# A state chunk's sums kept in one PSUM bank: A S added onto AK V, outputs onto R S, operand copied by ScalarE

## The chip, the cores and the metric

The kernel runs on one core of one Trainium2 chip. The metric is device time in microseconds (us) of one execution. Five engines with queues of their own take part: TensorE (PE in the profile, with its weight loads as PEld), VectorE (DVE), ScalarE (ACT), GpSimd (POOL) and SyncE (SP), which issues most transfers. Each runs its instructions in the order in which they stand in its queue. TensorE writes to PSUM, whose banks the kernel names by tags ("d" and "g" and "ry" two buffers each, "tr" and "sas" one each).

## The reference, cut to what matters

One layer takes an input of 1024 tokens by 1024 channels, projects it, and runs three branches: an RWKV-7 recurrence with 16 heads of 64 channels, a convolution of width 31, and a cross-attention into 256 memory tokens. The branches are merged by gates and projected again. The change lies in the recurrence, and in the group normalisation behind it:

```
def step(state, inp):
    r_t, w_t, k_t, v_t, a_t, b_t = inp
    sa = jnp.einsum('bhvk,bhk->bhv', state, a_t)
    state = (state * w_t[:, :, None, :]
             + sa[..., :, None] * b_t[:, :, None, :]
             + v_t[..., :, None] * k_t[:, :, None, :])
    y = jnp.einsum('bhvk,bhk->bhv', state, r_t)
    return state, y
...
mu = jnp.mean(wkv, axis=-1, keepdims=True)
var = jnp.mean(jnp.square(wkv - mu), axis=-1, keepdims=True)
wkv = ((wkv - mu) * lax.rsqrt(var + RWKV_GN_EPS)).reshape(B, S, RWKV_WIDTH)
```

## The kernel before

The recurrence is computed in chunks of 64 tokens. A tile j holds two heads (128 channels); its 1024 tokens are two halves e of 512, and a half is 8 chunks, in two quarters q of 4. In each chunk the kernel needs, besides products within the chunk, the state S (128x128, two heads on the diagonal) from the chunk before. The instructions come from four kinds of Python generators:

- tile jobs (`g_dense`, L298): the projections. A half tile is 24 matmuls with 512 columns into a "d" bank, then a few operations on it (L379 to L385, L427), the split of weights into a high and a low part (L123 on ScalarE, L124 on VectorE; `wh`, `wl`), and the load of the next weights.
- `g_prep`: decays, keys and queries of a half, with `ar` and `bk` as its results, and the products of the chunk against itself (L552, masked on VectorE by L555).
- `g_sub`: the inversion of a triangular matrix for all chunks of a half. The masked products go through DRAM (`ud`, L560, L573), GpSimd scales them (L581, `U`), and a loop of 31 steps on VectorE (L587 and L590, `W`) does the inversion; the result goes through DRAM again and becomes `TT`.
- `g_chain`: the recurrence over the 8 chunks of a half. In `g_pre`, per quarter, K and V are transposed (L640, L647, bank "tr"); AK V (L666) goes to the second half of that bank, and ScalarE copies it to `Y` (L675). Then, per chunk: R S and A S in one matmul (L709, `ry`), VectorE adds A S and AK V to `sav` (L710), ScalarE scales the old state (L713, `sp`), TensorE makes the update (L717, `sas`), VectorE joins both (L720, `s`). After four chunks the outputs' own part (L731, `yp`) goes to a "tr" bank, ScalarE copies it to `Y` (L733), VectorE adds R S (L738), and takes statistics (L742). At the end of a half, small operations (L750 to L755), a reciprocal square root on GpSimd (L114, L118, `vr`), two normalising operations (L760, L761), a transposition on TensorE (L766), two more VectorE operations (L768, L769) and a store.

`mix()` interleaves the generators, by the shares of their steps that are done, so that TensorE has projection matmuls between the steps of the recurrence. A compiler pass then gives every engine its order, by its own estimate of when things are ready; it is fixed when the kernel runs. So a change in one generator moves instructions of the others.

The stretch of the profile from about 60 to 990 us is this recurrence stage. It repeats with a period of one tile j, that is two chains (e = 0 and e = 1), some 114 us. The text calls "X" the half period from the transposition L766 that ends a chain e = 1 to the one that ends the chain e = 0 (in the period shown: 479.25 to 535.01 us), and "Y" the other half.

Of the kernel before, what the change touches and what calls it, by code (L numbers as in the profile page):

```python
# [13 lines left out]
ALU = mybir.AluOpType  # L14
# [4 lines left out]
P = 128  # L19
# [5 lines left out]
C = 64  # L25
# [7 lines left out]
RMS_EPS = 1e-6  # L33
LN_EPS = 1e-5
GN_EPS = 64e-5
PAIR_EVERY = 34.0
TAP = 1.4
LOS = (13, 14, 15, 16, 17)
# [24 lines left out]
def hybrid_kernel(ctx: ExitStack, tc: tile.TileContext, x: bass.AP, mem: bass.AP, wt: bass.AP,  # L63
                  vecs: bass.AP, wup: bass.AP, gfin: bass.AP, out: bass.AP):
    nc = tc.nc
    act, dve, pool, pe = nc.scalar, nc.vector, nc.gpsimd, nc.tensor
# [7 lines left out]
    def bank(tag, bufs=1):  # L74
        return ps.tile([P, HS], F32, name=tag, tag=tag, bufs=bufs)
# [37 lines left out]
    def rsqrt(out_ap, in_ap, mul, add):  # L113
        pool.tensor_scalar(out=out_ap, in0=in_ap, scalar1=mul, scalar2=add, op0=ALU.mult, op1=ALU.add)  # L114
        p0 = in_ap.shape[0]
        n = in_ap.shape[1]
        base = 0 if p0 == P else P - p0
        pool.tensor_tensor(out=out_ap, in0=out_ap, in1=nhalf[base:P, 0:n], op=ALU.pow)  # L118
# [63 lines left out]
    order = [kinds[n_] + j for lst, _ in schedule for n_, j in lst]  # L182


    def jb(name, *idx):
        return [(name, i) for i in idx]
# [9 lines left out]
    for job in rest[1:]:  # L196
        att_jobs.append(job)
        t_ += cost.get(job[0], 10.2)
        if npair < KT and t_ > npair * PAIR_EVERY:
            att_jobs += jb("gb", npair) + jb("ga", npair)  # L200
# [135 lines left out]
    with tc.tile_pool(name="rk", bufs=1, reuse_waits="tile") as rk:  # L336


        def so(par):
            return 0 if par else C  # L340

        def ko(par):
            return C if par else 0
# [46 lines left out]
        def fl(ap):  # L390
            return ap.rearrange("p a t -> p (a t)")
# [240 lines left out]

        state = [0]

        def g_pre(j, e, q, g, bk, v, Y):
            tkp = bank("tr")
            for cc in range(4):
                pe.transpose(tkp[:, cc * P:(cc + 1) * P], fl(bk[:, q * 4 + cc, :, :]), ident)  # L640
            tk = rk.tile([P, 4, P], F32, name="tk", tag="tk", bufs=2)
            act.copy(tk, tkp.rearrange("p (c t) -> p c t", t=P))
            yield
            vtp = bank("tr")
            for cc in range(2):
                c = q * 4 + cc * 2
                pe.transpose(vtp[:, cc * P:(cc + 1) * P], v[:, c * C:(c + 2) * C], ident)  # L647
            sav = rk.tile([P, 4, P], F32, name="sav", tag="sav", bufs=2)
            for par in range(2):
                rows = slice(ko(par), ko(par) + C)  # L650
                act.copy(sav[rows, par::2, :], vtp[rows, 0:2 * P].rearrange("p (c t) -> p c t", t=P))
            yield
            zv = vtp[:, 2 * P:4 * P]
            u1 = bank("g", 2)
            uv = u1.rearrange("p (k c h t) -> p k c h t", k=2, c=2, h=2)
            for n in range(4):
                cc2, hh = n // 2, n % 2
                vsl = slice(hh * C, (hh + 1) * C)
                for par in range(2):
                    own = slice(so(par), so(par) + C)  # L660
                    oth = slice(ko(par), ko(par) + C)
                    cc = cc2 * 2 + par
                    gc = g[:, par, hh, q * 2 + cc2]
                    pe.matmul(uv[own, 0, cc2, hh, :], lhsT=TT[own, hh * 4 + q * 2 + cc2, :], rhs=tk[own, cc, vsl],
                              start=True, stop=True)
                    pe.matmul(zv[own, n * C:(n + 1) * C], lhsT=gc[oth, own], rhs=sav[oth, cc, vsl],  # L666
                              start=True, stop=True)
            for n in range(4):
                cc2, hh = n // 2, n % 2
                for par in range(2):  # L670
                    own = slice(so(par), so(par) + C)
                    oth = slice(ko(par), ko(par) + C)
                    pe.matmul(uv[own, 1, cc2, hh, :], lhsT=TT[own, hh * 4 + q * 2 + cc2, :],
                              rhs=g[own, par, hh, q * 2 + cc2, oth], start=True, stop=True)
            act.copy(fl(Y[:, q * 2:q * 2 + 2, :]), zv)  # L675
            for par in range(2):
                own = slice(so(par), so(par) + C)
                oth = slice(ko(par), ko(par) + C)
                act.copy(tk[own, par::2, :], uv[own, 0].rearrange("p c h t -> p c (h t)"))
                act.copy(g[own, par, :, q * 2:q * 2 + 2, oth], uv[own, 1].rearrange("p c h t -> p h c t"))  # L680
            yield (tk, sav)

        def g_chain(j, e):
            g, ar, bk, pc = GG.pop((j, e)), AR.pop((j, e)), BK.pop((j, e)), PCS.pop((j, e))
            v = VS.pop((j, e))
            if e == 0:
                dve.memset(s0[state[0]], 0.0)

            Y = rk.tile([P, 4, P], F32, name="Y", tag="Y", bufs=1)
            st = rk.tile([P, 4, 2, 6], F32, name="st", tag="st", bufs=1)  # L690
            pre = [g_pre(j, e, q, g, bk, v, Y) for q in range(2)]
            got = None
            for got in pre[0]:
                yield
# [2 lines left out]
            bv = rk.tile([P, HS], F32, name="bv", tag="bv", bufs=1)  # L697
            dve.tensor_tensor(out=bv, in0=bp, in1=v, op=ALU.mult)
            for q in range(2):
                tk, sav = got  # L700
                ry = bank("ry", 2)
                for cc in range(4):
                    c = q * 4 + cc
                    par = c % 2
                    cg = e * CPH + c
                    own = slice(so(par), so(par) + C)
                    cs = slice(cc * P, (cc + 1) * P)
                    S0, S1 = s0[state[0]], s0[1 - state[0]]
                    pe.matmul(ry[:, cs], lhsT=fl(ar[:, c, :, :]), rhs=S0, start=True, stop=True)  # L709
                    dve.tensor_tensor(out=sav[own, cc, :], in0=ry[own, cs], in1=Y[own, c // 2, :], op=ALU.add)  # L710
                    if cg < NCH - 1:
                        sp = rk.tile([P, P], F32, name="sp", tag="sp", bufs=1)
                        act.activation(sp, S0, AF.Copy, scale=pc[:, c:c + 1])  # L713
                    yield
                    if cg < NCH - 1:
                        sn = bank("sas")
                        pe.matmul(sn[:, 0:P], lhsT=tk[:, cc, :], rhs=sav[:, cc, :], start=True, stop=True)  # L717
                        for hh in range(2):
                            vsl = slice(hh * C, (hh + 1) * C)
                            dve.scalar_tensor_tensor(out=S1[vsl, vsl], in0=sn[vsl, vsl], scalar=pc[vsl, c:c + 1],  # L720
                                                     in1=sp[vsl, vsl], op0=ALU.mult, op1=ALU.add)
                        state[0] = 1 - state[0]
                    if q == 0 and cc < 3:
                        got = next(pre[1])
                    yield
                yp = bank("tr")
                for n in range(4):
                    cc2, hh = n // 2, n % 2
                    for par in range(2):
                        oth = slice(ko(par), ko(par) + C)  # L730
                        pe.matmul(yp[oth, n * C:(n + 1) * C], lhsT=g[:, par, hh, q * 2 + cc2, oth],  # L731
                                  rhs=sav[:, cc2 * 2 + par, hh * C:(hh + 1) * C], start=True, stop=True)
                act.copy(fl(Y[:, q * 2:q * 2 + 2, :]), yp[:, 0:2 * P])  # L733
                yield
                ryv = ry.rearrange("p (c t) -> p c t", t=P)
                for par in range(2):
                    oth = slice(ko(par), ko(par) + C)
                    dve.tensor_tensor(out=Y[oth, q * 2:q * 2 + 2, :], in0=Y[oth, q * 2:q * 2 + 2, :],  # L738
                                      in1=ryv[oth, par::2, :], op=ALU.add)
                for c2 in range(q * 2, q * 2 + 2):  # L740
                    for hh in range(2):
                        dve.bn_stats(out=st[:, c2, hh, :], in_=Y[:, c2, hh * C:(hh + 1) * C])  # L742
                yield
# [11 lines left out]
            dve.scalar_tensor_tensor(out=vr, in0=df, scalar=16.0, in1=vr, op0=ALU.mult, op1=ALU.add)  # L755
            rsqrt(vr, vr, 1.0 / C, GN_EPS)
            for _ in range(GNW):
# [418 lines left out]
    with tc.tile_pool(name="wo1", bufs=1, reuse_waits="tile") as w1:  # L1176
# [12 lines left out]
        for fh in range(2):  # L1189
            fs = slice(fh * HS, (fh + 1) * HS)  # L1190
            oh, ol = wo[fh]
            for t in range(KT):
# [10 lines left out]
                if fh == 1:  # L1203
                    rsqrt(rs[:, t:t + 1], ss[:, t, 1:2], 1.0 / D, e0[:, t:t + 1])
                    for h_ in range(2):
                        hs_ = slice(h_ * HS, (h_ + 1) * HS)
                        dve.scalar_tensor_tensor(out=xr[t][:, hs_], in0=xr[t][:, hs_], scalar=rs[:, t:t + 1],
                                                 in1=gf[:, hs_], op0=ALU.mult, op1=ALU.mult)
# [46 lines left out]
```

## Time and profile before

| | before |
|---|---|
| runs | 1951.31, 1953.14, 1950.67 us; median 1951.31 |
| profiled execution | 1949.77 us, span 1947.8 us, granted clock 0.993 |
| PE busy | 1844.5 us, 95% |
| DVE busy | 1410.6 us, 72% |
| ACT busy | 691.9 us, 36% |
| POOL busy | 227.7 us, 12% |
| DMA, mean | 97 GB/s |

A table like this says which engine has the least room over the whole program. It does not say what a change in one stage is worth; for that the stage's own rows are read, which stand below.

### The profile page before, as it was taken

The page shows a single profiled execution, that of the slowest core. Times are in us where ns is not written, and L with a number is a line of the kernel's source. Part 1 is how long each engine was busy: PE and PEld are TensorE (multiplying, and loading weights), DVE is VectorE, ACT ScalarE, POOL GpSimd, SP SyncE. Part 2 cuts the span into 40 slices and gives each one's busy share as a digit, 9 for nine tenths or more (in the row PEclk, how much of TensorE's full clock was granted, in tenths as well). Part 3 has the DMA queues.
Part 4 walks back from the last instruction along what each step waited for, and adds up shares of the span by engine and source line. Part 5 has one row for each costly group of instructions (what it writes and reads, how often), then busy time and mean ns, then how long its engine had stood idle before and what let it go on. Part 6 is the DMA issues. An engine that isn't in the chain of part 4 may idle for free.

```text
span 1947.8 us, 30024 instructions
## 1 busy us (share of the span) xinstructions
PE 1844.5 (95%) x11412; PEld 1472.2 (76%) x11412; DVE 1410.6 (72%) x3028; ACT 691.9 (36%) x1303; POOL 227.7 (12%) x311
## 2 busy tenths in 40 slices
PE   6999998999899898998999999999999999899998
PEld 5777776766676676776788888888888788778886
DVE  5667787777878777787735998898999857654423
ACT  6334343433344343343333323131313335432121
POOL 2201111111111112111000000000000223100001
PEclk9999999999999999999999999999999999999999
DMA  4232212222121222212224411112122666785432
GB/s 147 57 99 58 77 35 63 60 56 74 42 83 44 62 63 53 77 42 71 69 72 141 130 54 55 65 59 71 44 76 87 227 199 214 246 283 170 129 130 86
DMA packets 127936, 188.61 MB, mean 97 GB/s; under 512 B 64432, under 2 KB 66608, under 8 KB 127792
## 3 DMA queue, kind: packets, MB, share of 16 engines
q1 hardware_dynamic: 122704, 178.11, 29.8%
q10 hardware_dynamic: 4768, 8.07, 1.1%
q8 instruction: 89, 1.46, 0.3%
q0 software_dynamic: 320, 0.52, 0.1%
q14 instruction: 55, 0.45, 0.1%
HBM read 139.92 MB, written 46.20 MB: 96 GB/s over the span
## 4 chain that ended last, share of the span: by engine, by line
PE 63%; DVE 23%; DMA 4%; issue 4%; ACT 3%; POOL 3%; SPq 0%; DVEq 0%; POOLq 0%; ACTq 0%
PE d L298 41%; PE g L298 5%; PE g L212 4%; DVE W L590 3%; DVE tm L587 3%; PE d L212 2%; DVE s L720 2%; PE g L552 2%; DVE wl L124 2%; DVE sav L710 1%; PE ry L894 1%; POOL vr L118 1%; DVE Y L761 1%; DVE Y L738 1%; PE sas L717 1%
## 5 line engine op out<-in xcount | busy, mean ns | idle before, releaser
L298 PE MATMUL d<-hH,wh 128*128 128x512 f32 x1504 | 607.2, 404 | 2.4 <-ACT lc L383 2.0
L298 PE MATMUL d<-hH,wl 128*128 128x512 f32 x1504 | 603.0, 401 | 0.0
L298 PE MATMUL d<-hL,wh 128*128 128x512 f32 x1504 | 600.1, 399 | 0.0
L298 PEld LDWEIGHTS d<-hH,wl 128*128 128x128 f32 x1504 | 285.0, 189 | 56.9
L298 PEld LDWEIGHTS d<-hH,wh 128*128 128x128 f32 x1504 | 285.3, 190 | 55.8 <-ACT lc L383 2.4
L298 PEld LDWEIGHTS d<-hL,wh 128*128 128x128 f32 x1504 | 285.0, 189 | 53.6
L848 DVE SCALAR_TENSOR_TENSOR ac<-up,wdw,ac 128x1024 f32<-128x1024 f32 x240 | 308.0, 1283 | 11.8 <-ACT ac L845 5.9
L123 ACT CAST wh<-wf 128x1024 fp32r<-128x1024 f32 x137 | 143.6, 1049 | 311.3 <-PE d L298 277.1
L124 DVE TENSOR_TENSOR wl<-wf,wh 128x1024 fp32r<-128x1024 f32 x137 | 177.6, 1296 | 83.8 <-ACT wh L123 83.3
L590 DVE TENSOR_TENSOR W<-W,tm 128x60 f32<-128x60 f32 (+24 forms) x496 | 112.3, 226 | 10.0
L587 DVE TENSOR_TENSOR tm<-W,U 128x60 f32<-128x60 f32 (+24 forms) x496 | 107.7, 217 | 11.1
L713 ACT ACTIVATE sp<-s,pc 128x128 f32<-128x128 f32 x120 | 48.3, 402 | 174.8 <-DVE s L720 137.6
L717 PEld LDWEIGHTS sas<-sav,tk 128*128 128x128 f32 x240 | 38.5, 188 | 67.7 <-DVE sav L710 49.4
L717 PE MATMUL sas<-sav,tk 128*128 128x128 f32 x240 | 54.2, 307 | 34.3 <-DVE sav L710 32.6
L720 DVE SCALAR_TENSOR_TENSOR s<-sas,pc,sp 64x64 f32<-64x64 f32 x240 | 67.6, 282 | 21.5 <-PE sas L717 16.1
L298 PE MATMUL g<-oH,wh 128*128 128x512 f32 x192 | 76.3, 398 | 5.3 <-ACT wh L123 5.3
L298 PE MATMUL g<-oH,wl 128*128 128x512 f32 x192 | 76.2, 397 | 2.1 <-DVE wl L124 2.1
L298 PE MATMUL g<-oL,wh 128*128 128x512 f32 x192 | 75.8, 395 | 0.0
L298 PE MATMUL d<-oL,wh 128*128 128x512 f32 x192 | 75.2, 392 | 0.0
L298 PE MATMUL d<-oH,wl 128*128 128x512 f32 x192 | 75.2, 392 | 0.0
L298 PE MATMUL d<-oH,wh 128*128 128x512 f32 x192 | 75.2, 392 | 0.0
L710 DVE TENSOR_TENSOR sav<-ry,Y 64x128 f32<-64x128 f32 x128 | 36.8, 287 | 43.7 <-ACT Y L675 26.8
(301 smaller groups left out, 2910.6 us busy)
## 6 DMA issues: line engine op xcount, KB each, us to landing
wf<-in_wt_dram SPq DMA_DIRECT2D x137, 512.0 KB
g_d<-gt SPq DMA_DIRECT2D x48, 256.0 KB
U<-ud SPq DMA_DIRECT2D x64, 128.0 KB
nxt<-in_x_dram SPq DMA_DIRECT2D x8, 512.0 KB
o_rwkv_d<-o SPq DMA_DIRECT2D x16, 256.0 KB
cv_d<-ac SPq DMA_DIRECT2D x8, 512.0 KB
o_mem_d<-om SPq DMA_DIRECT2D x16, 256.0 KB
xs<-cv_d SPq DMA_DIRECT2D x8, 512.0 KB
```

Source lines behind the costliest of these rows:

```text
L123: act.copy(hi, src)
L124: (eng or dve).tensor_tensor(out=lo, in0=src, in1=hi.bitcast(F32), op=ALU.subtract)
L212: pe.matmul(po, lhsT=l, rhs=r, start=(i == 0), stop=(i == n - 1))
L298: pe.matmul(po, lhsT=l[:, ks_], rhs=r[:, k, sl], start=(n == 0), stop=(n == 3 * KT - 1))
L552: pe.matmul(gps[hh][:, cc * P:(cc + 1) * P], lhsT=fl(bk[rows, c, :, :]), rhs=fl(ar[rows, c, :, :]), start=True, stop=True)
L587: dve.tensor_tensor(out=tv, in0=W[:, 0:m, i:i + 1].broadcast_to([NG * 32, m, n]), in1=U[:, i:i + 1, i + 1:32].broadcast_to([NG * 32, m, n] ...
L590: dve.tensor_tensor(out=wv_, in0=wv_, in1=tv, op=ALU.add)
L710: dve.tensor_tensor(out=sav[own, cc, :], in0=ry[own, cs], in1=Y[own, c // 2, :], op=ALU.add)
L713: act.activation(sp, S0, AF.Copy, scale=pc[:, c:c + 1])
L717: pe.matmul(sn[:, 0:P], lhsT=tk[:, cc, :], rhs=sav[:, cc, :], start=True, stop=True)
L720: dve.scalar_tensor_tensor(out=S1[vsl, vsl], in0=sn[vsl, vsl], scalar=pc[vsl, c:c + 1], in1=sp[vsl, vsl], op0=ALU.mult, op1=ALU.add)
L848: dve.scalar_tensor_tensor(out=ac, in0=up[:, tap:tap + S], scalar=wdw[:, tap * 8 + j:tap * 8 + j + 1], in1=ac, op0=ALU.mult, op1=ALU.add)
```

## The change

In `g_pre`, AK V (L671 of the changed kernel) goes into the `ry` bank and begins the sums there; R S and A S (L716) are added onto it; ScalarE copies A S + AK V to `sav` (L720, act.copy of 64x128), and VectorE's addition is gone. The outputs' own part (L741) is added onto R S in the same bank, and ScalarE copies the sum to `Y` in two pieces of 64x256 (L748); the copy of 128x256 and VectorE's two additions are gone, and so is the copy of AK V. The line numbers behind the first hunk are higher by 1 up to `g_pre`, and by up to 10 behind it. In all:

- removed: 128 additions of 64x128 and 64 of 64x256 on VectorE, 64 copies of 128x256 on ScalarE;
- added: 128 copies of 64x128 and 64 of 64x256 on ScalarE;
- the same matmuls, with other accumulation flags and order; the "tr" bank is used less.

```diff
-            zv = vtp[:, 2 * P:4 * P]
+            ry = bank("ry", 2)
+            first = {}
             u1 = bank("g", 2)
...
-                    pe.matmul(zv[own, n * C:(n + 1) * C], lhsT=gc[oth, own], rhs=sav[oth, cc, vsl],
-                              start=True, stop=True)
+                    mm = pe.matmul(ry[own, cc * P + hh * C:cc * P + (hh + 1) * C], lhsT=gc[oth, own],
+                                   rhs=sav[oth, cc, vsl], start=par not in first, stop=False,
+                                   skip_group_check=True)
+                    if par in first:
+                        tc.add_manual_dep(mm.ins, first[par].name, NOSYNC, reason="sums begun in order")
+                    else:
+                        first[par] = mm.ins
...
-            act.copy(fl(Y[:, q * 2:q * 2 + 2, :]), zv)
...
-                ry = bank("ry", 2)
...
-                    pe.matmul(ry[:, cs], lhsT=fl(ar[:, c, :, :]), rhs=S0, start=True, stop=True)
-                    dve.tensor_tensor(out=sav[own, cc, :], in0=ry[own, cs], in1=Y[own, c // 2, :], op=ALU.add)
+                    mm = pe.matmul(ry[:, cs], lhsT=fl(ar[:, c, :, :]), rhs=S0, start=False, stop=False,
+                                   skip_group_check=True)
+                    for begun in first.values():
+                        tc.add_manual_dep(mm.ins, begun.name, NOSYNC, reason="sums begun in order")
+                    act.copy(sav[own, cc, :], ry[own, cs])
...
-                yp = bank("tr")
...
-                        pe.matmul(yp[oth, n * C:(n + 1) * C], lhsT=g[:, par, hh, q * 2 + cc2, oth],
-                                  rhs=sav[:, cc2 * 2 + par, hh * C:(hh + 1) * C], start=True, stop=True)
-                act.copy(fl(Y[:, q * 2:q * 2 + 2, :]), yp[:, 0:2 * P])
+                        cc = cc2 * 2 + par
+                        pe.matmul(ry[oth, cc * P + hh * C:cc * P + (hh + 1) * C],
+                                  lhsT=g[:, par, hh, q * 2 + cc2, oth], rhs=sav[:, cc, hh * C:(hh + 1) * C],
+                                  start=False, stop=True, skip_group_check=True)
...
-                    dve.tensor_tensor(out=Y[oth, q * 2:q * 2 + 2, :], in0=Y[oth, q * 2:q * 2 + 2, :],
-                                      in1=ryv[oth, par::2, :], op=ALU.add)
+                    act.copy(Y[oth, q * 2:q * 2 + 2, :], ryv[oth, par::2, :])
```

The change moves instructions on every engine. Three places matter for what follows. The first is ScalarE's queue in X, where the first chunk of the chain's second quarter stands (`lc` is a 128x1 operation of a tile job, which needs VectorE's L380 before it). Before:

```order
L713 ACTIVATE sp<-s_1_406,pc 128x128
L495 ACTIVATE e_412<-lw 128x8x64
L496 ACTIVATE lw<-lw 128x512
L733 COPY Y<-tr 128x256
L491 ACTIVATE ta_5194<-g,a0h 128x512
L379 ACTIVATE rs<-d,omm 128x512
L383 ACTIVATE lc<-d,vec 128x1
L123 CAST hsh<-rs 128x512
```

With the change:

```order
L723 ACTIVATE sp<-s_1_406,pc 128x128
L496 ACTIVATE e_412<-lw 128x8x64
L497 ACTIVATE lw<-lw 128x512
L748 COPY Y<-ry 64x256
L492 ACTIVATE ta_5155<-g,a0h 128x512
L748 COPY Y<-ry 64x256
L380 ACTIVATE rs<-d,omm 128x512
L384 ACTIVATE lc<-d,vec 128x1
L720 COPY sav<-ry 64x128
L124 CAST hsh<-rs 128x512
```

The copy of `sav` of that chunk, which was an addition in VectorE's queue, now stands on ScalarE behind `lc`, and the two copies of `Y` stand apart.

The second is GpSimd's queue at the end of Y. Before:

```order
L574 MEMSET W 128x256
L580 COPY W<-rb 32x8 x4
L581 TENSOR_TENSOR U<-U,rb 128x1024
L114 TENSOR_SCALAR vr<-vr 128x8
L118 TENSOR_TENSOR vr<-vr,nhalf 128x8
```

With the change:

```order
L575 MEMSET W 128x256
L581 COPY W<-rb 32x8 x4
L115 TENSOR_SCALAR vr<-vr 128x8
L119 TENSOR_TENSOR vr<-vr,nhalf 128x8
L582 TENSOR_TENSOR U<-U,rb 128x1024
```

The scaling of `U` moved behind the reciprocal square root in Y; in X it stood behind it already.

The third is VectorE's queue at the end of X. Before:

```order
L738 TENSOR_TENSOR Y<-Y,ry 64x256 x2
L742 BN_STATS st<-Y 128x6 x4
...
L754 TENSOR_TENSOR df<-df 128x8
L124 TENSOR_TENSOR wl<-wf,wh 128x1024
L755 SCALAR_TENSOR_TENSOR vr<-df,vr 128x8
L760 TENSOR_TENSOR Y<-Y,mn 128x512
L428 SCALAR_TENSOR_TENSOR sg<-sg,d 128x512
L761 TENSOR_TENSOR Y<-Y,vr 128x512
L768 SCALAR_TENSOR_TENSOR o<-tr,vec,bv 128x512
```

With the change:

```order
L751 BN_STATS st<-Y 128x6 x4
...
L763 TENSOR_TENSOR df<-df 128x8
L769 TENSOR_TENSOR Y<-Y,mn 128x512
L764 SCALAR_TENSOR_TENSOR vr<-df,vr 128x8
L770 TENSOR_TENSOR Y<-Y,vr 128x512
L556 TENSOR_TENSOR g<-g,cmask_390 128x512 x2
L777 SCALAR_TENSOR_TENSOR o<-tr,vec,bv 128x512
L125 TENSOR_TENSOR wl<-wf,wh 128x1024
```

The weights' split `wl` moved from in front of the normalisation to behind it, and the second pair of masks, which stood before the chain's last additions, now stands behind the normalisation too; the transfers of `U` wait for these masks.

## Rows read from the trace of the kernel before

**Rows 1.** Windows: start:end, length, busy us of PE, PEld, DVE, ACT, POOL; clock; DMA.

```profile
461.00:575.00 114.00, 104.34 (x848) 79.19 (x847) 90.24 (x280) 45.23 (x97) 16.94 (x26) 1.00 0.23 61
1150.00:1200.00 50.00, 50.00 (x245) 42.38 (x244) 40.40 (x37) 10.75 (x15) 3.30 (x2) 1.00 0.21 64
```

**Rows 2.** Waits of TensorE from 100 to 960 us: total, times, longest.

```profile
PE sas L717 <- DVE sav L710: 32.6, 43, 1.9
PE tr L766 <- DVE Y L761: 19.1, 6, 3.2
PE tr L766 <- DVE W L590: 6.2, 6, 1.0
PE ry L709 <- DVE s L720: 5.8, 13, 0.9
```

**Rows 3.** Timeline of TensorE, 501 to 507 us.

```profile
503.78 0.49 PE L717 MATMUL sas<-sav,tk 128*128 128x128 f32 x2 [0.87 <-DVE sav L710]
...
504.33 0.39 PE L298 MATMUL d<-hL,wh 128*128 128x512 f32 x1
504.56 0.40 PE L298 MATMUL d<-hH,wl 128*128 128x512 f32 x1
```

**Rows 4.** Timeline of VectorE, same place.

```profile
501.16 0.75 DVE L380 SCALAR_TENSOR_TENSOR rs<-d,vec,rs 128x511 f32<-128x511 f32 x1
...
503.43 0.29 DVE L710 TENSOR_TENSOR sav<-ry,Y 64x128 f32<-64x128 f32 x1
```

**Rows 5.** Timeline of ScalarE, same place.

```profile
501.94 0.26 ACT L383 ACTIVATE lc<-d,vec 128x1 f32<-128x1 f32 x1 [1.25 <-DVE rs L380]
```

**Rows 6.** Timeline of VectorE at the end of X.

```profile
532.05 2.82 DVE L761 TENSOR_TENSOR Y<-Y,vr 128x512 f32<-128x512 f32 x1 [1.10 <-POOL vr L118]
```

**Rows 7.** Timeline of GpSimd at the end of X.

```profile
530.37 1.64 POOL L118 TENSOR_TENSOR vr<-vr,nhalf 128x8 f32<-128x8 f32 x1
531.98 2.34 POOL L581 TENSOR_TENSOR U<-U,rb 128x1024 f32<-128x1024 f32 x1
```

**Rows 8.** Timeline of VectorE at the end of Y.

```profile
469.54 3.02 DVE L124 TENSOR_TENSOR wl<-wf,wh 128x1024 fp32r<-128x1024 f32 x1 [2.86 <-ACT wh L123]
...
473.62 0.85 DVE L738 TENSOR_TENSOR Y<-Y,ry 64x256 f32<-64x256 f32 x2 [0.33 <-ACT Y L733]
474.50 0.61 DVE L742 BATCH_NORM_STATS2 st<-Y 128x6 f32<-128x64 f32 x4
...
478.41 0.69 DVE L761 TENSOR_TENSOR Y<-Y,vr 128x512 f32<-128x512 f32 x1 [1.94 <-POOL vr L118]
```

**Rows 9.** Window behind a long TensorE wait.

```profile
420.50:423.90 3.40, 3.40 (x11) 2.73 (x10) 1.28 (x2) 1.18 (x2) 0.00 (x0) 0.50 0.38 98
```

**Rows 10.** VectorE's lines, 100 to 960 us: busy, mean ns, idle before.

```profile
L590 DVE TENSOR_TENSOR W<-W,tm 128x60 f32<-128x60 f32 (+24 forms) x486 | 110.4, 227 | 9.7
...
L710 DVE TENSOR_TENSOR sav<-ry,Y 64x128 f32<-64x128 f32 x116 | 33.3, 287 | 33.7 <-ACT Y L675 26.8 <-PE ry L709 4.1
```

**Rows 11.** ScalarE's lines, 100 to 960 us.

```profile
L679 ACT COPY tk<-g 64x256 f32<-64x256 f32 x60 | 22.0, 367 | 1.4
```

**Rows 12.** Timeline of TensorE: products of a quarter grouped by kind, and what follows.

```profile
482.56 0.68 PE L664 MATMUL g<-tk,TT 64*64 64x64 f32 x16
...
484.14 0.50 PE L461 MATMUL g<-hsh,bones 128*128 128x512 f32 x1
```

**Rows 13.** Timeline of TensorE: the same products in turn, and what follows.

```profile
549.39 0.27 PE L664 MATMUL g<-tk,TT 64*64 64x64 f32 x1
...
550.48 0.50 PE L298 MATMUL d<-hH,wh 128*128 128x512 f32 x1
```

**Rows 14.** Timeline of VectorE: the last masks of Y.

```profile
572.25 1.29 DVE L555 TENSOR_TENSOR g<-g,cmask 128x512 f32<-128x512 f32 x2 [0.86 <-PE g L552]
```

**Rows 15.** Timeline of GpSimd behind those masks.

```profile
581.94 2.38 POOL L581 TENSOR_TENSOR U<-U,rb 128x1024 f32<-128x1024 f32 x1 [4.87 <-DMA U<-ud]
```

**Rows 16.** Timeline of TensorE: the products that VectorE masks.

```profile
520.51 1.16 PE L552 MATMUL g<-ar,bk 64*128 64x128 f32 x14
```

More of the change, by code (lines that the diff above doesn't have):

```diff
@@ L35 @@
 GN_EPS = 64e-5
+NOSYNC = mybir.DependencyInfo(mybir.DependencyClass.NoSync, mybir.DependencyReason.DATA)
 PAIR_EVERY = 34.0
@@ L635, in hybrid_kernel, with g_pre @@
         state = [0]
-        def g_pre(j, e, q, g, bk, v, Y):
+        def g_pre(j, e, q, g, bk, v):
             tkp = bank("tr")
@@ L680, in g_pre @@
                 act.copy(g[own, par, :, q * 2:q * 2 + 2, oth], uv[own, 1].rearrange("p c h t -> p h c t"))
-            yield (tk, sav)
+            yield (tk, sav, ry, first)
         def g_chain(j, e):
@@ L690, in g_chain @@
             st = rk.tile([P, 4, 2, 6], F32, name="st", tag="st", bufs=1)
-            pre = [g_pre(j, e, q, g, bk, v, Y) for q in range(2)]
+            pre = [g_pre(j, e, q, g, bk, v) for q in range(2)]
             got = None
@@ L699, in g_chain @@
             for q in range(2):
-                tk, sav = got
-                ry = bank("ry", 2)
+                tk, sav, ry, first = got
                 for cc in range(4):
```

## The prediction

> **What bounds the kernel now.** I read the windows first, because a share over the whole program mixes stages. In one period of the recurrence stage TensorE is busy 104.34 of 114.00 us; in a later stage it is busy all of the time [rows 1]. So there are 9.66 us per period that a change on other engines can give back or add to, and the stage has some 7.5 periods (from 100 to 960 us, at 114 us each). VectorE, with 90.24 us, has the highest load of those that feed TensorE; ScalarE has 45.23 [rows 1].
>
> Next come TensorE's waits [rows 2]: for `sav`, 32.6 us, 4.3 per period; for the normalised `Y` at the transposition in X, 19.1 in 6 waits, 3.2 each; for the same transposition in Y, 6.2 in 6, 1.0 each; for the new state, 5.8, 0.8 per period. Together that is 9.3 per period, nearly all of the idle time. The timeline shows what a wait for `sav` looks like: the update at 503.78 waited 0.87 [rows 3], since the addition of 0.29 us ran only at 503.43, behind other work of VectorE [rows 4]. Four projection matmuls, 0.23 us apart [rows 3], stand between R S and the update; 0.9 us hides a prompt operation, but not one that queues.
>
> **The change: VectorE.** A period has 16 chunks and 4 quarters. VectorE loses 16 additions of 287 ns [rows 10], 4.6 us, and 8 of 0.42 us (two took 0.85 [rows 8]), 3.4 us: 8.0 of its 90.24. This is worth only what it takes out of TensorE's waits.
>
> **ScalarE.** Of a copy of 64x128 from PSUM the trace shows none. It is more than the 0.26 us of an operation of one column [rows 5] and less than the 0.367 of a copy of 64x256 [rows 11]; I take 0.31. So 16 copies add 5.0 us, and 8 copies into `Y` at 0.367 replace 8 larger ones of about the same time. ScalarE goes from 45 to about 50 of 114 us: no bound by itself. With the bounds it is 49.4 to 51.1.
>
> **The waits for `sav`, 4.3 before.** A copy takes about as long as the addition did, so the gain is in queueing: ScalarE is idle 56% of the time, VectorE 21%. But ScalarE also works in order. In X's fifth chunk the copy now stands behind `lc`, which waited 1.25 us for VectorE's L380 [rows 5]; behind `lc` stand the copy, the cast of `rs`, and all of ScalarE's later work. The wait there was 0.87 [rows 3]; it is at least 0, if L380 comes earlier, and at most 0.87 + 1.25 = 2.1. I take 1.5, nearer to the upper end, since L380 stays in the more loaded queue. Y's fourth chunk has its copy behind four copies of the next quarter's products; between 0 and the longest wait seen, 1.9 [rows 2], I take 0.9, the middle. The 14 other chunks find the copy at once or behind one operation: 0.4 in all. Sum 2.8, with 0.4 to 4.4 as ends.
>
> **The transposition, 4.2 before.** From the start of the statistics at 474.50 to the start of the last normalising operation at 478.41 there are 3.91 us [rows 8]. Ahead of it now come two overlapping copies, 0.65, where the additions took 0.88; behind it the last operation, 0.69 if undisturbed [rows 8], and some 0.1 to TensorE. That makes 5.4. The queue of TensorE holds 20 projection matmuls (4.6 us) behind the chain's last products in either half, and in X eight masked products as well, 1.16 x 16/14 = 1.3 by [rows 16], where each counts as two records. So X is covered by 5.9, and its wait of 3.2 goes to about 0. This also needs that the last operation is not disturbed: in X before it took 2.82 instead of 0.69, while GpSimd scaled `U` beside it [rows 6, 7], and in Y the split of weights took 3.02 beside the same scaling [rows 8]. In X the masks that `U` waits for now stand behind this operation, so the scaling comes later. In Y the scaling has moved behind the reciprocal square root. From the end of the masks (573.54) to the scaling (581.94) there were 8.4 us [rows 14, 15], and the reciprocal square root ends some 11 us behind these masks, counted along TensorE's queue with the same durations; so `U` is there, and the scaling starts just as the last operation does. With 2.82 there, and `lc` between Y's two copies (0.4), the path is 0.65 + 0.4 + 3.91 + 2.82 + 0.1 = 7.9 against a cover of 4.6: a wait of 3.3 where there was 1.0. If it doesn't collide, 1.2. So the large wait is handed from X to Y, and the sum goes from 4.2 to 3.3.
>
> **The waits for the state, 0.8 before.** At three chunks (X's seventh, Y's sixth and seventh) the joining `s` now stands behind the rest of the inversion loop or behind a pair of masks, which takes 1.29 [rows 14]. Between 0 and 1.29 each, I take 0.8: it must be more than the shortest cover of four matmuls to show at all. Sum 2.4, with 0 to 3.9 as ends.
>
> **TensorE itself.** The quarters' products took 1.58 us where they stood grouped by kind, 482.56 to 484.14 [rows 12], and 1.09 where the two kinds alternated, 549.39 to 550.48 [rows 13]. Before, two of a period's four quarters were grouped; after, none is: -1.0 us. The projections are cut into three more pieces per period, each with a slower first matmul, about 0.09: +0.3. The bank "tr" comes free sooner, which I count at nothing, as no wait on it is in [rows 2]; against it stand small waits behind the later masks, +0.3.
>
> **The sum per period:** 9.3 goes to 2.8 + 3.3 + 2.4 + 0.3 = 8.8, then -1.0 + 0.3; in all -1.2. Times 7.5 that is -9 us. Behind a long transposition wait a stretch of 3.40 us at a granted clock of 0.50, the 1.2 GHz level, follows [rows 9], which costs about half of it, 1.7; as one wait of over 3 us per period stays, I change nothing there. From the profiled execution's 1949.8 (span 1947.8 and 2.0 around it) I get 1940.8; the median of the runs is 1.5 higher, so the forecast is 1942. A difference of 0.2%, 3.9 us, is about what a measurement of this kernel can tell from none.
>
> **Rival 1, slower: the scaling of `U` at the start of Y holds VectorE.** Since X's masks now come behind the normalisation, `U` is scaled about 9.5 us behind the transposition (8.4 by [rows 14, 15] after masks that end some 1 us behind it), and takes 2.3 [rows 7]. The inversion loop's first operation waits for it, in order, and behind that stand nine loop operations of about 0.22 [rows 10], two larger ones, and the second chunk's `s`. This `s` then ends some 14.8 us behind the transposition; by the same counting (projection matmuls at 0.23, products at 1.1) TensorE asks for it at about 15.9. The slack is 1.1. If one operation beside the scaling is stretched as [rows 6, 8] show, by 2.1, the slack is gone, and the two chunks that follow are late too. At 2.1 per period the time is 1942 + 16 = 1958. It decides from 1.2 us per period on. For it: the collision is in the rows twice per period. Against it: now there are more projection matmuls in front of that chunk. The Trainium skill, GPSIMD Engine Reference, Specifications, says that the SBUF interfaces which GpSimd shares with VectorE are contended by VectorE instructions with two SBUF inputs (or in a 2-port mode). The trace agrees with both of its stretched operations, 2.82 and 3.02 us; by that rule the scan and the low parts at Y's start would be held, and `s`, which reads PSUM, only behind them, which is this rival's 1958.
>
> **Rival 2, much faster: the new waits are hidden.** If VectorE, with 8 us less to do, and ScalarE are prompt at every chunk, then of 8.8 only Y's 3.3 stays: -5.5 x 7.5 = -41, or 1901. With half of that, 1922. For it: the waits that I expect at single chunks are taken from the middle of their bounds. Against it: the copies and `s` stay behind in-order neighbours that wait for other engines.
>
> **Rival 3, no change.** Waits move from VectorE's queue to ScalarE's and from X to Y in full, 1947 to 1955. **Rival 4, slower: ScalarE's queue decides.** If every copy waits 0.3 us behind a long cast beyond its cover, 16 x 0.3 = 4.8 per period, the time is 1942 + 36 = 1978. It is against the load of 44%.
>
> **How the numbers follow.** The forecast with its near neighbours, 1932 to 1947: 0.30. Rival 2, below 1932: 0.23. No change: 0.17. Rival 1: 0.25. Rival 4: 0.05. So faster 0.53, same 0.17, slower 0.30. The range leaves out the far half of rival 2 and rival 4 with the far end of rival 1: 1920 to 1961.
>
> **What would show it.** After the change the wait for `Y` at the transposition should be near 0 in X and some 3 us in Y, with the last normalising operation in Y near 2.8 us and GpSimd's scaling beside it. Waits for `sav` should be released by ScalarE, some 2.8 per period, the longest at X's fifth chunk, behind `lc`. Waits for `s` should be near 2.4. VectorE should lose about 8 us per period, ScalarE gain about 5. A wait of over 1 us at Y's third chunk, with the loop waiting for `U`, would be rival 1. The prediction is wrong if waits for `sav` stay near 4 or fall to 1, or if Y's collision doesn't happen.

## The result, and the profile after

The changed kernel takes 1923.18 us (median of 5 runs, 1920.71 to 1934.38) against 1951.31 before; the ratio is 0.9859, with a 95% interval of 0.9842 to 0.9876. That is 27.5 us by the ratio, three times the 9 us of the forecast, in the forecast's direction, and the time of its second rival with half of that rival's effect.

The profiled execution of the changed kernel is the slowest of the five, 1934.4 us; the other four took 1920.7 to 1924.2, at a mean clock of 0.990 to 0.994 instead of 0.985. Its stretches at half clock are taken out below where totals are compared. The busy line of its page:

```profile
PE 1832.7 (95%) x11412; PEld 1477.4 (76%) x11412; DVE 1367.1 (71%) x2836; ACT 732.1 (38%) x1431; POOL 234.8 (12%) x311
```

VectorE lost 43.5 us and ScalarE gained 40.2. Next the windows (columns as in [rows 1]), one period without a half-clock stretch, and the 3.2 us a little behind the wait that ends it:

```profile
804.30:914.80 110.50, 101.05 (x846) 78.29 (x846) 85.05 (x254) 49.91 (x112) 17.87 (x26) 1.00 0.23 61
916.00:919.20 3.20, 3.20 (x11) 2.58 (x10) 3.16 (x7) 0.59 (x1) 0.00 (x0) 0.52 0.17 42
```

This period takes 110.5 us where one without half clock took 114.0 [rows 1]. TensorE's idle time in it is 9.45, against 9.66: nearly the same. So 3.3 of the 3.5 us came out of time in which TensorE counts as busy, which is the puzzle of this case. The second row is the clock: it falls to its half level behind the transposition's wait, as in [rows 9].

TensorE's waits from 100 to 960 us:

```profile
PE ry L716 <- DVE s L730: 23.4, 27, 2.1
PE tr L775 <- DVE Y L770: 22.3, 7, 3.2
PE sas L727 <- ACT sav L720: 18.0, 19, 1.3
```

Their sum is 63.7 us, and that of [rows 2] is 63.7 as well. The waits for `sav` fell from 32.6 to 18.0, now released by ScalarE; those for the state rose from 5.8 to 23.4; the transposition in X waits no more, and in Y 3.2 us each time.

The timeline of TensorE shows what the idle time leaves out (start, duration, idle before):

```profile
832.70 0.40 PE L299 MATMUL d<-hH,wl 128*128 128x512 f32 x1
834.27 0.49 PE L727 MATMUL sas<-sav,tk 128*128 128x128 f32 x2 [1.17 <-ACT sav L720]
834.51 0.48 PE L299 MATMUL d<-hH,wh 128*128 128x512 f32 x1
...
837.56 0.39 PE L299 MATMUL d<-hH,wl 128*128 128x512 f32 x1
837.79 0.38 PE L727 MATMUL sas<-sav,tk 128*128 128x128 f32 x2
837.93 0.48 PE L299 MATMUL d<-hH,wh 128*128 128x512 f32 x1
```

The update at 837.79 starts 0.23 behind the matmul ahead of it, and the next starts 0.14 later: 0.37 in all. The one at 834.27 waited. From 832.70 to 834.51 are 1.81 us, 1.44 more than 0.37, but its idle time is given as 1.17. The other 0.27 counts as busy: the end of the matmul ahead, which otherwise lies beside the next one, and the two passes of the update, which start 0.10 further apart. A wait that is shorter than this end has no idle time at all in the profile and still costs.

So I summed, for each kind of instruction, the time from the start of the one ahead to its own start, from 60 us to the last transposition. Half-clock time is half of the time from the start to the next start for projection matmuls that lasted over 550 ns; it depends by some 0.2 us on that limit. "Waited" are instructions whose passes start over 150 ns apart.

| us | before | after |
|---|---|---|
| stage, 60 us to the last transposition | 975.2 | 957.1 |
| half-clock time in it | 6.2 | 13.3 |
| updates: sum / idle / waited of 120 | 93.3 / 34.3 / 84 | 66.8 / 18.3 / 28 |
| R S: sum / idle / waited of 128 | 57.1 / 6.2 / 49 | 75.9 / 23.4 / 36 |
| transposition of Y: sum | 38.9 | 34.4 |
| products of the quarters: sum | 47.7 | 41.0 |
| projections without half-clock time | 571.6 | 569.6 |
| all others | 160.3 | 156.1 |

Without half-clock time the stage went from 969.0 to 943.8: 25.2 us. Behind the stage the two kernels differ by less than 0.5 us, if the half-clock time there is taken off in the same way.

ScalarE's line for the new copy, and the two timelines at X's fifth chunk and Y's end:

```profile
L720 ACT COPY sav<-ry 64x128 f32<-64x128 f32 x119 | 30.8, 259 | 60.5 <-PE ry L716 55.9
```

```profile
833.67 0.26 ACT L384 ACTIVATE lc<-d,vec 128x1 f32<-128x1 f32 x1 [0.89 <-DVE rs L381]
833.96 0.26 ACT L720 COPY sav<-ry 64x128 f32<-64x128 f32 x1
```

```profile
865.84 2.88 DVE L125 TENSOR_TENSOR hsl<-kk,hsh 128x512 fp32r<-128x512 f32 x1
...
911.97 2.82 DVE L770 TENSOR_TENSOR Y<-Y,vr 128x512 f32<-128x512 f32 x1 [2.12 <-POOL vr L119]
```

```profile
865.71 2.46 POOL L582 TENSOR_TENSOR U<-U,rb 128x1024 f32<-128x1024 f32 x1 [10.23 <-DMA U<-ud]
...
911.89 2.35 POOL L582 TENSOR_TENSOR U<-U,rb 128x1024 f32<-128x1024 f32 x1
```

The copy stands behind `lc` as the order had shown, and lets TensorE wait 1.17. The scaling of `U` meets VectorE twice per period. In Y it meets the last normalising operation, which takes 2.82 or 2.83 in each of seven periods. After X it meets a different one from period to period: `hsl` in the period shown (2.88), the scan L494 in two (2.69 instead of 1.23), L488 in three:

```profile
529.90 2.04 DVE L488 TENSOR_SCALAR lw<-lw 128x512 f32<-128x512 f32 x1
```

```profile
529.28 2.39 POOL L582 TENSOR_TENSOR U<-U,rb 128x1024 f32<-128x1024 f32 x1 [9.37 <-DMA U<-ud]
```

In the one period left the scan keeps its 1.23, and the scaling takes 3.37. The normalising operation, `hsl` and the scan have two inputs in SBUF, and the Trainium skill, GPSIMD Engine Reference, Specifications, names VectorE instructions with two SBUF inputs, or in a 2-port mode, as those that contend with GpSimd for SBUF; the trace agrees for these three. L488 has one input, takes 0.42 elsewhere, and no run shows its mode.

### The profile page after: what moved, and what is told of

The parts are those of the page before. It is cut to its first block, busy times and chain, and to the rows that moved or that the text cites. A ratio compares the mean times of both kernels' runs of the same rounds, so it can differ in the third digit from the quotient of the medians.

```text
span 1932.5 us, 29812 instructions
## 1 busy us (share of the span) xinstructions
PE 1832.7 (95%) x11412; PEld 1477.4 (76%) x11412; DVE 1367.1 (71%) x2836; ACT 732.1 (38%) x1431; POOL 234.8 (12%) x311
## 4 chain that ended last, share of the span: by engine, by line
PE 61%; DVE 24%; DMA 5%; issue 3%; ACT 3%; POOL 2%; SPq 1%; DVEq 0%; POOLq 0%; ACTq 0%
PE d L299 40%; PE g L299 6%; DVE W L591 4%; DVE tm L588 4%; PE g L213 3%; PE d L213 2%; DVE s L730 2%; DVE wl L125 2%; DVE ac L857 2%; PE g L553 1%; DVE Y L770 1%; PE ry L213 1%; DVE lw L494 1%; DMA xv<-cv_d 1%; PE ry L903 1%
## 5 line engine op out<-in xcount | busy, mean ns | idle before, releaser
L299 PEld LDWEIGHTS d<-hH,wl 128*128 128x128 f32 x1504 | 286.1, 190 | 57.1
L125 DVE TENSOR_TENSOR wl<-wf,wh 128x1024 fp32r<-128x1024 f32 x137 | 170.3, 1243 | 65.7 <-ACT wh L124 65.1
L588 DVE TENSOR_TENSOR tm<-W,U 128x60 f32<-128x60 f32 (+24 forms) x496 | 103.8, 209 | 15.6 <-POOL U L582 2.2
L716 PEld LDWEIGHTS ry<-s,ar 128*128 128x128 f32 x256 | 43.9, 188 | 47.4 <-DVE s L730 41.3
L716 PE MATMUL ry<-s,ar 128*128 128x128 f32 x256 | 52.9, 288 | 23.4 <-DVE s L730 23.4
L727 PEld LDWEIGHTS sas<-sav,tk 128*128 128x128 f32 x240 | 42.9, 189 | 38.8 <-ACT sav L720 31.0
```

What stands on the lines that cost most here:

```text
L125: (eng or dve).tensor_tensor(out=lo, in0=src, in1=hi.bitcast(F32), op=ALU.subtract)
L299: pe.matmul(po, lhsT=l[:, ks_], rhs=r[:, k, sl], start=(n == 0), stop=(n == 3 * KT - 1))
L588: dve.tensor_tensor(out=tv, in0=W[:, 0:m, i:i + 1].broadcast_to([NG * 32, m, n]), in1=U[:, i:i + 1, i + 1:32].broadcast_to([NG * 32, m, n] ...
L716: mm = pe.matmul(ry[:, cs], lhsT=fl(ar[:, c, :, :]), rhs=S0, start=False, stop=False, skip_group_check=True)
```

## The experiments

The theory after the result: the gain is the number of updates that wait, not the idle time beside them; it comes from ScalarE being prompt, and VectorE's freed time is needed for it. Rivals: the gain is in TensorE's own order (products that alternate), in the bank "tr", or only in one half of the change. The ratios are to the kernel before, timed on the same chip; 0.9859 is the changed kernel's.

**1. VectorE makes the copy to sav.**

```diff
-                    act.copy(sav[own, cc, :], ry[own, cs])
+                    dve.tensor_copy(sav[own, cc, :], ry[own, cs])
```

> The changed kernel, but VectorE makes the copy to sav (64x128 out of ry) that ScalarE makes there; all the rest of the change stays. Theory: the larger part of the gain is that the update no longer queues for sav behind VectorE's other work; then the updates that wait rise from 28 of 120 towards the 84 of before, and the time goes from 1923 to 1932 to 1942. Rival: the engine of this copy is worth nothing, and the gain comes from the sums in one bank (no copies of AK V, products that alternate, two additions fewer); then the time stays within 4 us of 1923.

Ratio 0.9936 (0.9918 to 0.9954), 1940 us. TensorE's waits:

```profile
PE sas L727 <- DVE sav L720: 45.9, 47, 2.0
PE tr L775 <- DVE Y L770: 13.2, 7, 1.9
PE ry L716 <- DVE s L730: 4.8, 15, 1.0
```

82 of 120 updates wait, and 42 R S. Summed as in the table, updates and R S take 161.1 us instead of 142.7, the transposition 24.5 instead of 34.4. So the copy's engine, with the order that comes with it, is worth some 15 us, 18 at the chunks: the theory's side.

**2. The products of a quarter one kind behind the other.**

```diff
+            for n in range(4):
...
                     mm = pe.matmul(ry[own, cc * P + hh * C:cc * P + (hh + 1) * C], lhsT=gc[oth, own],
```

> The changed kernel with the eight products AK V of a quarter written behind the eight products TT K instead of in turn with them; the same matmuls. Theory: the two kinds use different quarters of TensorE and run side by side only where they alternate, so that each of 32 quarters takes about 0.5 us more (1.58 against 1.09 as in the rows of before), and the time goes from 1923 to 1935 to 1940. Rival: it was not the order but the wait for the copy of V that made these stretches long before; then the time stays within 4 us of 1923.

Ratio 0.9859 (0.9833 to 0.9884): no difference. A quarter on TensorE's timeline, and what follows:

```profile
470.45 0.51 PE L668 MATMUL g<-tk,TT 64*64 64x64 f32 x10
...
471.65 0.50 PE L299 MATMUL d<-hH,wh 128*128 128x512 f32 x1
```

It takes 1.20 us, not 1.58 as in [rows 12]. So my reason falls: it was not the grouping. In the kernel before, ScalarE's copy of V for the quarter of [rows 12] is this row:

```profile
482.67 0.74 ACT L651 COPY sav<-tr 64x256 f32<-64x256 f32 x2 [0.56 <-PE tr L647]
```

It ended at 483.41, and the first product AK V started at 483.47:

```profile
483.47 0.51 PE L666 MATMUL tr<-sav,g 64*64 64x64 f32 x10
```

The quarter was long because it held a short wait, again without idle time in the profile; in the changed order three projection matmuls stand ahead of the quarter.

**3 and 4. Each half of the change alone.** In 3 the outputs stay as before (`yp` in a bank "tr", a copy, two additions); in 4 AK V stays with its copy and VectorE's additions, and only the outputs are added onto R S. From the edit of 3:

```diff
-                    mm = pe.matmul(ry[:, cs], lhsT=fl(ar[:, c, :, :]), rhs=S0, start=False, stop=False,
+                    mm = pe.matmul(ry[:, cs], lhsT=fl(ar[:, c, :, :]), rhs=S0, start=False, stop=True,
...
+                yp = bank("tr")
...
+                    dve.tensor_tensor(out=Y[oth, q * 2:q * 2 + 2, :], in0=Y[oth, q * 2:q * 2 + 2, :],
+                                      in1=ryv[oth, par::2, :], op=ALU.add)
```

> Half of the change: AK V and A S in one bank and sav copied by ScalarE, as in the changed kernel; the outputs as before (products into a bank tr, a copy of 128x256 by ScalarE, two additions by VectorE). Theory: this half carries the gain (waits for sav, alternating products), so 1920 to 1932. Rival: the relief of VectorE and of the bank tr by the outputs' part matters as much; then 1937 to 1945.

> The other half: AK V copied by ScalarE and added by VectorE to A S as before; the outputs' products added onto R S in ry, and ScalarE copies the sum to Y in two pieces. Theory: this half alone gives little, 1943 to 1952, since the waits for sav stay as they were. Rival: it gives half of the gain or more, 1925 to 1938.

The sums alone: 1.0031 (1.0018 to 1.0043), slower than before. The outputs alone: 0.9950 (0.9934 to 0.9967). The two add up to about -0.2%; together they give -1.4%. Both of my expectations for the sums' half were wrong; that the outputs' half alone gives little was expected. The waits of the sums' half:

```profile
PE ry L716 <- DVE s L730: 33.9, 32, 2.7
PE tr L776 <- DVE Y L771: 25.0, 10, 3.8
PE sas L727 <- ACT sav L720: 12.6, 15, 1.3
```

Waits for `sav` fall to 12.6, as far as one could wish, and the waits for the state take it all back: 33.9 instead of 5.8. This fits VectorE's queue, with the outputs' additions still in it, being met one matmul later. With the outputs alone, the waits for `sav` even rise:

```profile
PE sas L718 <- DVE sav L711: 47.9, 48, 2.1
PE tr L766 <- DVE Y L761: 13.2, 7, 1.9
```

**5. VectorE copies the sums to Y.**

```diff
-                    act.copy(Y[oth, q * 2:q * 2 + 2, :], ryv[oth, par::2, :])
+                    dve.tensor_copy(Y[oth, q * 2:q * 2 + 2, :], ryv[oth, par::2, :])
```

> The changed kernel, but VectorE makes the 64 copies of 64x256 from the sums to Y; the sums in one bank and ScalarE's copy to sav stay. Theory: the outputs' half of the change pays through VectorE's time (some 3 us per period, in front of the chain's end and of the new states), and the half that moves sav pays only where VectorE has that time free; then waits for the new state grow from 23 to about 30 us, and the time goes to 1932 to 1945. Rival: it pays through the bank tr, which the outputs no longer pass; then the time stays at 1919 to 1928.

Ratio 0.9976 (0.9950 to 1.0002), 1945.5 us: at the upper end of what the theory had. The bank "tr" is as free as in the changed kernel, and the gain is gone all the same; VectorE is busy for 1394.8 us, 28 more. Its first wait:

```profile
PE ry L716 <- DVE s L730: 34.8, 34, 2.4
```

**6. Work of VectorE that nobody waits for.**

```diff
+                    junk = rk.tile([P, 6], F32, name="junk", tag="junk", bufs=1)
+                    dve.bn_stats(out=junk[own, :], in_=ry[own, cs])
```

> The changed kernel, and besides 128 statistics operations of VectorE (64x128 out of ry, about as long as the removed additions), behind each R S, whose result nobody reads. Theory: VectorE's time by itself costs in this stage, because the new states, the inversion loop and the normalisation stand behind it; then these 35 us of unused work cost 10 to 20 us, 1933 to 1943, about as much as the run in which VectorE makes the copy to sav. Rival: only work that someone waits for costs; then the time stays at 1921 to 1927, and that run's loss was the place of the copy in VectorE's queue.

Ratio 0.9916 (0.9900 to 0.9933), some 11 us above the changed kernel, for this line:

```profile
L722 DVE BATCH_NORM_STATS2 junk<-ry 64x6 f32<-64x128 f32 x119 | 35.1, 295 | 5.9 <-ACT sav L720 2.9
```

So VectorE's time costs by itself in this stage, about a third of a us for each us. Waits for the state rose from 23.4 to 35.5. How much of the 15 us of run 1 is the same cost stays open: there the waits for the state fell to 4.8, and those for `sav` rose.

**7 to 11. The transposition's wait, and what VectorE's freed time is worth.** Run 7 lets VectorE scale `U`. Run 8 puts the transposition two steps of the chain later. Run 9 does the same to the kernel before. Run 10 does 7 and 8. Run 11 is run 8 with one step.

```diff
-            pool.tensor_tensor(out=U, in0=U, in1=rb[:, None, :].broadcast_to([NG * 32, 32, 32]), op=ALU.mult)
+            dve.tensor_tensor(out=U, in0=U, in1=rb[:, None, :].broadcast_to([NG * 32, 32, 32]), op=ALU.mult)
```

```diff
-            for _ in range(GNW):
+            for _ in range(GNW + 2):
...
-        n_steps = {"dense": 12, "prep": 13, "sub": 20 + SUBW, "chain": CHN + 2 * GNW}
+        n_steps = {"dense": 12, "prep": 13, "sub": 20 + SUBW, "chain": CHN + 2 * GNW + 2}
```

> The changed kernel, but the scaling of U (128x1024) is made by VectorE and not by GpSimd. Theory: the wait of 3.2 us at Y's transposition comes from the last normalising operation being stretched from 0.7 to 2.8 us by GpSimd's scaling beside it; without that the waits there fall from 22 to under 9 us in all, with fewer stretches at half clock behind them, against 2.4 us more work on VectorE per period; 1905 to 1917. Rival: VectorE now waits in its queue for U itself, and holds the new states behind it; 1925 to 1945.

> The changed kernel with the transposition two steps of the chain later (28 projection matmuls and 32 to 48 small products between the chain's last products and the transposition, instead of 20 and 0 to 8). Theory: Y's path of some 8 us is then covered, its wait of 3.2 us goes to nothing, and with it the stretches at half clock; 1898 to 1910. Rival: the next chain starts later by as much and its waits for the new state take the time back; 1917 to 1928.

Run 7: 0.9759 (0.9743 to 0.9774), 1901 us, below what the theory had. Run 8: 0.9744 (0.9729 to 0.9758), 1898.5 us, no different from run 7 within the intervals. Both take the transposition off the list. The waits of run 7:

```profile
PE ry L716 <- DVE s L730: 33.1, 35, 1.9
PE sas L727 <- ACT sav L720: 13.2, 15, 1.2
PE tr L616 <- DVE TT L608: 3.3, 6, 0.7
```

The waits of run 8 are all here:

```profile
PE ry L716 <- DVE s L730: 30.8, 36, 1.7
PE sas L727 <- ACT sav L720: 15.6, 29, 1.1
```

The last normalising operation in Y, in run 7, in run 8 and in run 11:

```profile
451.39 0.69 DVE L770 TENSOR_TENSOR Y<-Y,vr 128x512 f32<-128x512 f32 x1 [2.12 <-POOL vr L119]
```

```profile
453.68 0.69 DVE L770 TENSOR_TENSOR Y<-Y,vr 128x512 f32<-128x512 f32 x1 [2.12 <-POOL vr L119]
```

```profile
462.79 2.83 DVE L770 TENSOR_TENSOR Y<-Y,vr 128x512 f32<-128x512 f32 x1 [2.12 <-POOL vr L119]
```

Run 7 shows that the collision with GpSimd's scaling was the price at Y's transposition. Run 8 was meant to cover that price, but in its order the scaling comes behind the operation, so that the collision is gone there too, and the cover's own worth isn't separated from it. Half-clock time in the stage, 13.3 us in the changed kernel, is 1.1 in run 8 and 4.2 in run 7, where six stretches of 3.41 us follow shorter waits, such as this one:

```profile
435.74 0.49 PE L716 MATMUL ry<-s,ar 128*128 128x128 f32 x2 [1.87 <-DVE s L730]
```

```profile
436.40:439.80 3.40, 3.40 (x21) 2.42 (x20) 0.63 (x2) 0.13 (x1) 0.00 (x0) 0.50 0.49 119
```

> The kernel before, without the change, with the transposition two steps of the chain later as in the run with more cover. Theory: this takes only the transposition's waits (25 us) and some stretches at half clock; 1951 goes to 1918 to 1930, so that the change is worth 20 to 30 us with the cover as without it. Rival: the gain of the later transposition belongs to the changed kernel (whose queues have room); before stays at 1935 to 1950.

Run 9: 1.0184 (1.0162 to 1.0207), slower, which neither side expected. Its waits:

```profile
PE sas L717 <- DVE sav L710: 33.0, 29, 2.8
PE ry L709 <- DVE s L720: 27.7, 28, 1.3
PE tr L615 <- DVE TT L607: 21.9, 12, 3.3
```

The transposition's wait is gone, and the end of the inversion (`TT`, VectorE) is late instead, up to 3.3 us, with 33 us of half-clock time. In run 8 this wait is not there. With the later transposition the change is worth 0.9744 / 1.0184, that is 4.3%.

> The changed kernel with the later transposition and, besides, the scaling of U made by VectorE. Theory: both remove the same wait, so the second brings nothing more and its 2.4 us of VectorE's time per period delay the new states; 1898 to 1912. Rival: GpSimd's scaling still stretches VectorE's operations elsewhere, and the two gains add up in part; 1882 to 1895.

> The changed kernel with the transposition one step later instead of two (24 projection matmuls and 16 to 24 small products behind the chain's last products). Theory: the cover, some 6.5 us, leaves about 1.4 us of Y's path open; 1903 to 1913. Rival: one step does as much as two, as the new states' waits are shorter; 1893 to 1901.

Run 10: 0.9736 (0.9721 to 0.9750), as run 8: the two remove the same wait, as the theory had it, and both by removing the collision. Run 11: 0.9883 (0.9866 to 0.9899), no better than the changed kernel, which both sides missed. Two of its waits:

```profile
PE ry L716 <- DVE s L730: 32.6, 40, 2.6
PE tr L775 <- DVE Y L770: 17.8, 7, 2.6
```

One step takes only 0.6 us off the wait of 3.2, and the waits for the state rise by 9. The collision is still there in each of seven periods (2.83 above). I had treated Y's path as fixed, but what stands on VectorE and beside it moves with the order.

## Why the prediction was wrong

The mechanisms were there; the sum was mis-sized. By the terms of the prediction, for the stage (its 7.5 periods), against the table:

| term | predicted us | measured us |
|---|---|---|
| idle at updates and R S | +0.8 | +1.1 |
| what those waits cost beside their idle time | 0, not counted | -8.9 |
| transposition | -6.8 | -4.5 |
| products of the quarters | -7.5 | -6.7 |
| projections cut into more pieces | +2.3 | -2.0 |
| small waits; all other instructions | +2.3 | -4.2 |
| sum | -8.9 | -25.2 |

**The step that failed** is the one that took a wait's price from its idle time. The prediction said that idle time would hardly change, from 9.3 to 8.8 us per period, and it didn't (63.7 us before and after, 8.5 in each of 7.5 periods; 9.3 came from dividing the transposition's waits by six). But a wait costs up to 0.27 us besides, and 133 waiting updates and R S became 64. With 8.9 of the 16.3 us between forecast and result it is the largest term that was missed. The prediction itself held the hint, that four matmuls hide a prompt operation but not one that queues; it priced only the long waits.

**Second**, I gave the other small instructions and the bank "tr" nothing or a loss, because no wait on them was listed. There too time went that the idle time does not show (transpositions of K -1.7, head sums -1.6, masked products -1.1, and others). These, and the projections, make 10.8 us between forecast and result, against which the transposition and the products gave 3.1 less than forecast. That these small sums are short waits is likely but not shown.

**Right in kind and size:** X's transposition to 0 and Y's to 3.2 (3.3 predicted), with the collision at 2.82; the wait behind `lc`, 1.17 (1.5); waits for the state, 23.4 in 7.5 periods, 3.1 each (2.4); ScalarE's gain per period, 4.7 (5). **Right in sum with some luck:** waits for `sav`, 2.4 each (2.8), of which some 1.0 is Y's second chunk, which the forecast did not have. **Off in size:** VectorE's loss is 5.2, not 8. GpSimd meets its operations more often: from 461 to 577 us the means of L488, L542 and L523 (one line less before) rise from 0.42, 0.98 and 0.48 to 1.24, 1.30 and 0.61, where GpSimd works beside them. **Right in size for the wrong reason:** the products of the quarters, as run 2 shows.

**The rivals.** Rival 1's collision did happen at Y's start, and at its price. In the period with `hsl` at 2.88, the second chunk's update and the third chunk's R S wait:

```profile
872.00 0.49 PE L727 MATMUL sas<-sav,tk 128*128 128x128 f32 x2 [1.31 <-ACT sav L720]
...
874.97 0.49 PE L716 MATMUL ry<-s,ar 128*128 128x128 f32 x2 [0.41 <-DVE s L730]
```

From the start of the matmul ahead to that of the next, these two take 2.7 to 3.2 us together in seven periods, 2.9 in the mean (1.2 to 1.4 before), and the same two in X, which do not wait, 0.8: a cost of 2.1 per period, as the rival named it, and some 1.6 more than before. In run 7, without GpSimd's scaling, they take 1.3. So the kernel is faster although this rival came true; it was outweighed. Rival 2's half, 1922, is the measured time, but by luck: its mechanism, that the listed waits go, did not happen. What it named as the cause, VectorE's freed time and ScalarE's promptness, does matter (runs 1, 5, 6).

**What stays open.** Each of these kernels was ordered anew, so that a run changes more places than its edit. That the halves don't add up is measured; that VectorE's time matters follows from runs 5 and 6, and run 9 fits it, but how much of each ratio is an accident of the order is not separated.

## What to carry to other kernels

Price a wait from start to start, against the same instruction where it did not wait: idle time left out a part of every wait here, and the whole of the short ones. When an operation is moved from a loaded engine to a free one, ask which instruction meets the loaded engine's queue next: here the wait for the operand only moved to the new state, until the same engine was relieved of other work too. And when a change has freed an engine, look again at the cover that was set before: two steps more cost 1.8% before the change and gained 1.2% after it, where they also moved the scaling out of the way.

## What the runs showed of the hardware

From the start of the matmul ahead to that of the next, an update of 128x128 in two passes that waited took 0.64 us besides its idle time (834.27); one that did not took 0.37 (837.79). A copy of 64x128 from PSUM took ScalarE 259 ns, as long as an operation of 128x1 (0.26). GpSimd's scaling of some 2.4 us stretched the operation of VectorE that started beside it by most of its own length: the normalising one from 0.69 to 2.82, `hsl` from 0.68 to 2.88, and L488, with a single SBUF input, from 0.42 to between 2.04 and 2.42; where the scan had started first, the scaling took 3.37 instead. Stretches at half clock followed waits of 3.2 us at the transposition, but also waits of 1.6 to 1.9 in run 7.
